# Encoder layer on one core: the norm of the tile two ahead moved in front of the copies of a tile's value product

## The chip, the cores and the metric

The kernel runs on one core of one Trainium2 chip. Its time is the device time of one execution in microseconds (us), and lower is better. A core has a matrix engine (TensorE, PE in the rows; PEld is its weight loads), VectorE (DVE), ScalarE (ACT), GpSimd (POOL), and SyncE (SP), which here only issues transfers. Each engine takes its instructions strictly in the order in which they were given to it, and waits at an instruction until what it needs is there.

## The reference

One layer of a hybrid encoder in float32, with 2048 rows of 1024 features:

```python
h = rms_norm(x, attn_norm_g)
q, k, v, xr, gr = split(h @ w_in)            # 512 columns each
attn = diff_attention(q, k, v, ...)          # 4 heads
lru  = recurrent_group(xr, gr, ...)          # RG-LRU in both directions
x = x + concat(attn, lru) @ w_out
x = x + (gelu(g) * u) @ w_down               # [g | u] = DWConv3(rms_norm(x) @ w_up)
return rms_norm(x, final_norm_g)

def rms_norm(x, g):
    return x * rsqrt(mean(x * x, axis=-1) + 1e-6) * g
```

The change is in the first line, in the `v` part of the second, and nowhere else.

## The kernel before

`phase1` computes the normed rows, their transposes, and the five projections; `phase2` is the attention, `phase3` the output projection, and the classes `Up` and `Down` the feed-forward part. The change is in the first stage of `phase1`, the value projection, which takes 16 tiles of 128 rows.

For each tile t there are four steps. `load_x(t)` fetches 128x1024 values into one of two buffers `xt`. `norm(t)` squares and sums them on ACT (L93), scales the sum on DVE (L94), raises it to the power -1/2 on POOL (L96), and multiplies `xt` in place by that and by the gain on DVE (L138). `transposed(t)` turns the normed tile with eight PE transposes (L144) and splits the result for a product in three parts: `hT_hi` on ACT (L75) and the remainder `hT_lo` on DVE (L78). `values(t)` multiplies: 8 blocks of 3 matmuls (L81 to L83) into one PSUM tile `ps`; then `vh` is copied from it on ACT (L75), `vl` is the remainder on DVE (L78), and both go to DRAM (L160).

The loop runs ahead. Half way through the product of tile t, between its fourth and fifth block, `values` calls `mid`, which is `transposed(t + 1)`. After the whole of `values(t)` comes `norm(t + 2)`. So between the transposes of tile t+1 and those of tile t+2 PE has 24 matmuls: the second half of product t and the first half of product t+1.

In this stage PE, DVE and ACT keep the order in which the code was written (`manual_schedule`, L174); SP and POOL are ordered by the scheduler. `xt` has two buffers, so the load of tile t+2 waits until the transposes of tile t have read theirs. `vl` has one buffer, so the next `vl` waits until the last one is in DRAM. The last tiles also carry the first weights of the next projection: `split_w` (a cast on DVE, L77, and a subtraction on POOL, L78).

Of the kernel before, what the change touches and what calls it, by code (L numbers as in the profile page):

```python
# [22 lines left out]
NT = S // P  # L23
# [19 lines left out]
def encoder_layer(ctx, tc, x, w_qkr, w_v, w_out, w_up, w_down, w_a, w_x, par, lams, g_attn, g_ffn, g_fin, out):  # L43
# [3 lines left out]
    def pool_of(name, **kw):  # L47
        return tc.tile_pool(name=name, reuse_waits="tile", **kw)
# [24 lines left out]
    def split(hi, lo, src, hi_eng=A, lo_eng=V):  # L73
        if hi_eng is A:
            A.activation(out=hi, in_=src, func=AF.Copy)  # L75
        else:
            hi_eng.tensor_copy(hi, src)  # L77
        lo_eng.tensor_tensor(out=lo, in0=src, in1=hi, op=ALU.subtract)  # L78

    def mm3(ps, lh, ll, rh, rl, first, last):  # L80
        T.matmul(ps, lh, rh, start=first, stop=False)  # L81
        T.matmul(ps, lh, rl, start=False, stop=False)  # L82
        T.matmul(ps, ll, rh, start=False, stop=last)  # L83

    def keep_clock(ps, n):

        for _ in range(n):
            T.matmul(ps, ident, ident, start=True, stop=True)

    def rms_norm(xt, g_b, junk, pool):  # L90

        ss = pool.tile([P, 1], F32, name="ss", tag="ss")
        A.activation(out=junk, in_=xt, func=AF.Square, accum_out=ss)  # L93
        V.tensor_scalar(out=ss, in0=ss, scalar1=1.0 / D, scalar2=EPS, op0=ALU.mult, op1=ALU.add)  # L94
        r = pool.tile([P, 1], F32, name="r", tag="r")
        G.tensor_tensor(out=r, in0=ss, in1=mhalf[:, 0:1], op=ALU.pow)  # L96
        return r


    def phase1():  # L100
# [9 lines left out]
        def fetch_w(i):  # L110
            ws = wp.tile([P, KD, P], F32, name="ws", tag="ws", bufs=1)
            nc.sync.dma_start(ws, w_qkr[i])
            return ws

        def split_w(ws):
            wh = wp.tile([P, KD, P], F32R, name="wh", tag="wh")
            wl = wp.tile([P, KD, P], F32R, name="wl", tag="wl")
            split(wh, wl, ws, hi_eng=V, lo_eng=G)
            return wh, wl

        with ExitStack() as ea:
            pa = ea.enter_context(pool_of("p1a", bufs=2, side="right"))
            pv = ea.enter_context(pool_of("p1v", bufs=1, side="right"))
            pt = ea.enter_context(pool_of("p1t", bufs=2, space=PSUM))
            g_b = pv.tile([P, D], F32, name="g_b")
            wv_hi = pv.tile([P, KD, AW], F32R, name="wv_hi")
            wv_lo = pv.tile([P, KD, AW], F32R, name="wv_lo")
            junk = pv.tile([P, D], BF16, name="junk")
            xts = {}

            def load_x(t):
                xts[t] = pa.tile([P, D], F32, name="xt", tag="xt")
                nc.sync.dma_start(xts[t], x[t * P:(t + 1) * P, :])

            def norm(t):
                xt = xts[t]
                r = rms_norm(xt, g_b, junk, pa)
                V.scalar_tensor_tensor(out=xt, in0=xt, scalar=r, in1=g_b, op0=ALU.mult, op1=ALU.mult)  # L138

            def transposed(t):  # L140
                xt = xts.pop(t)
                tp = pt.tile([P, KD, P], F32, name="tp", tag="tp")
                for k in range(KD):
                    T.transpose(tp[:, k, :], xt[:, k * P:(k + 1) * P], ident)  # L144
                c, o = divmod(t * P, CH)
                split(hT_hi[c][:, :, o:o + P], hT_lo[c][:, :, o:o + P], tp, hi_eng=A if t else V)

            def values(t, mid=None):
                c, o = divmod(t * P, CH)
                ps = pp.tile([P, AW], F32, name="ps", tag="ps")  # L150
                for k in range(KD):
                    if mid and k == KD // 2:
                        mid()
                    mm3(ps, hT_hi[c][:, k, o:o + P], hT_lo[c][:, k, o:o + P], wv_hi[:, k, :], wv_lo[:, k, :],
                        k == 0, k == KD - 1)
                vh = pa.tile([P, AW], F32R, name="vh", tag="vh")
                vl = pa.tile([P, AW], F32R, name="vl", tag="vl", bufs=1)
                split(vh, vl, ps)
                for d_, s_ in zip(v_d, (vh, vl)):
                    nc.sync.dma_start(d_[:, :, t, :], s_.bitcast(F32).rearrange("p (h e) -> p h e", h=NH))  # L160

            load_x(0)
            nc.scalar.dma_start(g_b, g_attn.partition_broadcast(P))

            staged = []
            for kk, tag in zip(range(0, KD, 2), ("wh", "wh", "wl", "ws")):
                ws = wp.tile([P, 2, AW], F32, name="wvs", tag=tag, bufs=1 if tag == "ws" else 2)
                (nc.sync, nc.scalar)[kk // 2 % 2].dma_start(ws, w_v[:, kk:kk + 2, :])
                staged.append(ws)
            load_x(1)  # L170
            nc.scalar.dma_start(prm, par)

            first = ExitStack()
            first.enter_context(tc.manual_schedule(engines={mybir.EngineType.PE, mybir.EngineType.DVE,  # L174
                                                            mybir.EngineType.Activation}))
            idle = pt.tile([P, KD, P], F32, name="tp", tag="tp")[:, 0, :]

            def wv_high(i):
                A.activation(out=wv_hi[:, 2 * i:2 * i + 2, :], in_=staged[i], func=AF.Copy)

            def wv_low(i):
                V.tensor_tensor(out=wv_lo[:, 2 * i:2 * i + 2, :], in0=staged[i], in1=wv_hi[:, 2 * i:2 * i + 2, :],
                                op=ALU.subtract)

            keep_clock(idle, 22)
            norm(0)
            wv_high(0)
            wv_low(0)
            wv_high(1)
            transposed(0)  # L190
            keep_clock(idle, 5)
            wv_high(2)
            wv_high(3)
            wv_low(1)
            norm(1)
            wv_low(2)
            wv_low(3)
            for t in range(NT):
                if t + 2 < NT:
                    load_x(t + 2)  # L200
                values(t, (lambda: transposed(t + 1)) if t + 1 < NT else None)
                if t + 2 < NT:
                    norm(t + 2)
                if t == NT - 6:
                    ws = fetch_w(8)
                if t == NT - 3:
                    ready[8] = split_w(ws)
            first.close()
# [1064 lines left out]
    class Down(Steps):  # L1273
# [128 lines left out]
        def run(self, es):  # L1402
# [19 lines left out]
            self.last_rest()  # L1422

    phase1()
    kp_stack = ExitStack()
    kp = kp_stack.enter_context(pool_of("kp", bufs=2, side="right"))
# [78 lines left out]
```

## Time and profile before

| | |
|---|---|
| median of 3 runs | 2670.63 us (2669.95 to 2675.54) |
| the profiled execution | 2676.15 us, span 2674.4 us |
| PE busy | 2588.6 us, 97% of the span |
| DVE, ACT, POOL busy | 74%, 50%, 22% |
| value projection, from the first transposes to the end of the last product | about 9.4 to 136.4 us |

The profile is of one execution on the chip. A row names the line of the kernel, the engine, the operation, and what is written and read. Matmuls are pipelined: the next one starts before the one before it has ended, and the ends shown are modelled, so the distance from start to start says more than the duration. "Idle before" is the time in which the engine had nothing to do just before a row, with what ended it.

### The profile page before, as it was taken

To read this page: it belongs to the slowest core of one execution; us is meant where nothing else is said; L and a number is where in the kernel's file an instruction comes from. 1 tells how busy PE (TensorE), PEld (TensorE's weight loads), DVE (VectorE), ACT (ScalarE), POOL (GpSimd) and SP (SyncE) were. 2 spreads that over 40 slices of the span, in tenths; PEclk is the share of its full clock that TensorE was granted. 3 is DMA by queue.
4 is the path that set the end of the run, shared out by engine and by line. 5 is a ranking of instruction groups with operands and counts; after the bars stand their busy time and mean duration, and the time that the engine had idled before them with its cause. 6 is when DMAs were issued, how large, how long until landed. Compare 5 with 4: busy or idle time off the path is not lost. (4 is left out here: it accounts for less than half of the span.)

```text
span 2674.4 us, 33695 instructions
## 1 busy us (share of the span) xinstructions
PE 2588.6 (97%) x13018; PEld 2107.5 (79%) x13018; DVE 1976.9 (74%) x2487; ACT 1342.3 (50%) x1732; POOL 588.3 (22%) x488
## 2 busy tenths in 40 slices
PE   8899999999999999999989999989999998999998
PEld 6687788778888887877768888878888886878786
DVE  4445535579999999744388888898888777675876
ACT  3334534568888888732254444454444443332433
POOL 0113223146766666810000000000000000101100
PEclk9999999999999999999999999999999999999999
DMA  5421221240202001243453434354565344755743
GB/s 170 127 81 67 85 71 63 81 158 23 88 25 87 23 25 33 80 154 126 158 173 128 148 118 157 119 168 167 221 242 205 123 140 120 202 132 125 230 157 126
DMA packets 146018, 329.36 MB, mean 123 GB/s; under 512 B 18624, under 2 KB 74688, under 8 KB 137024
## 3 DMA queue, kind: packets, MB, share of 16 engines
q1 hardware_dynamic: 133632, 283.82, 30.7%
q0 software_dynamic: 11504, 41.42, 6.3%
q8 instruction: 102, 1.67, 0.3%
q10 hardware_dynamic: 720, 1.95, 0.2%
q14 instruction: 60, 0.49, 0.1%
HBM read 198.16 MB, written 128.97 MB: 122 GB/s over the span
## 5 line engine op out<-in xcount | busy, mean ns | idle before, releaser
L1003 ACT ACTIVATE wg<-sw 128x1024 fp32r<-128x1024 f32 (+1 forms) x136 | 140.7, 1034 | 397.9 <-PE q L1029 219.2
L1044 DVE TENSOR_TENSOR u<-q,u 128x512 f32<-128x512 f32 x340 | 234.4, 690 | 138.4 <-PE q L1029 134.1
L458 ACT ACTIVATE e<-e,mn 128x2048 f32<-128x2048 f32 x128 | 256.3, 2008 | 11.9 <-DVE mn L453 11.9
L449 PE MATMUL sc<-ks,qt 64*128 64x512 f32 x1536 | 229.9, 412 | 6.9 <-DVE mn L453 6.7
L1189 DVE SCALAR_TENSOR_TENSOR acc<-u,prm,acc 128x1023 f32<-128x1023 f32 (+1 forms) x176 | 226.0, 1284 | 9.8 <-ACT acc L1181 5.4
L469 DVE SCALAR_TENSOR_TENSOR e<-e,rc,e 128x1024 f32<-128x1024 f32 x128 | 211.4, 1652 | 2.3
L83 PE MATMUL ps<-hT_hi,wl 128*128 128x512 f32 x512 | 199.5, 390 | 0.0
L82 PE MATMUL ps<-hT_lo,wh 128*128 128x512 f32 x512 | 199.5, 390 | 0.0
L81 PE MATMUL ps<-hT_hi,wh 128*128 128x512 f32 x512 | 199.5, 390 | 0.0
L449 PEld LDWEIGHTS sc<-ks,qt 64*128 64x128 f32 x1536 | 147.9, 185 | 46.7 <-DVE mn L453 10.0
L1008 DVE TENSOR_TENSOR wg<-sw,wg 128x1024 fp32r<-128x1024 f32 (+1 forms) x136 | 161.9, 1190 | 27.6 <-ACT wg L1003 27.6
L1008 DVE TENSOR_TENSOR wg<-wr,wg 128x512 fp32r<-128x512 f32 (+3 forms) x136 | 126.9, 933 | 67.1 <-ACT wg L1003 67.1
L1003 ACT ACTIVATE wg<-wr 128x512 fp32r<-128x512 f32 (+3 forms) x136 | 111.7, 822 | 117.3 <-PE q L1029 103.7
L453 DVE CUSTOM_DVE_ANT_0 e<-sc,strip,mn 128x1024 f32<-128x1024 f32 x128 | 159.1, 1281 | 15.5 <-PE sc L449 14.7
L78 POOL TENSOR_TENSOR wTl<-wg,wTh 128x1024 fp32r<-128x1024 f32 x64 | 156.9, 2451 | 0.0
L1294 POOL DMA_DIRECT2D b15f<-in_w_down_dram x1 | 0.8, 814 | 704.6 <-DVE u L1102 704.6
L453 DVE CUSTOM_DVE_ANT_0 e<-sc,strip 128x1024 f32<-128x1024 f32 x128 | 150.9, 1214 | 5.6 <-PE sc L449 3.4
L1029 PE MATMUL q<-b14r,wg 128*128 128x512 f32 x440 | 150.0, 398 | 2.9 <-ACT u L1051 2.9
L1029 PE MATMUL q<-b0r,wg 128*128 128x512 f32 x448 | 151.3, 394 | 0.7 <-DVE wg L1008 0.7
L78 POOL TENSOR_TENSOR wTl<-wf,wTh 128x512 fp32r<-128x512 f32 x64 | 126.9, 1983 | 110.4 <-ACT wTh L75 107.7
L1029 PE MATMUL q<-b12r,wg 128*128 128x512 f32 x440 | 149.7, 398 | 0.0
L475 PEld LDWEIGHTS tp<-ident,e 128*128 128x128 f32 x1024 | 112.1, 142 | 45.5 <-ACT wTh L75 18.7
(320 smaller groups left out, 6668.9 us busy)
## 6 DMA issues: line engine op xcount, KB each, us to landing
wr<-in_w_up_dram SPq DMA_DIRECT2D x66, 512.0 KB, 5.5
s_d<-sw SPq DMA_DIRECT2D x22, 1024.0 KB, 4.8
sw<-s_d SPq DMA_DIRECT2D x22, 1024.0 KB, 4.8
a_d<-acc SPq DMA_DIRECT2D x154, 128.0 KB, 1.9
x_d<-u POOLq DMA_DIRECT2D x32, 512.0 KB, 5.4
wr<-a_d SPq DMA_DIRECT2D x32, 512.0 KB, 4.8
xt<-in_x_dram SPq DMA_DIRECT2D x30, 512.0 KB, 4.7
ws<-in_w_qkr_dram SPq DMA_DIRECT2D x16, 512.0 KB, 3.4
```

Source lines behind the costliest of these rows:

```text
L78: lo_eng.tensor_tensor(out=lo, in0=src, in1=hi, op=ALU.subtract)
L81: T.matmul(ps, lh, rh, start=first, stop=False)
L82: T.matmul(ps, lh, rl, start=False, stop=False)
L449: T.matmul(self.sc[c][:, n * CH:(n + 1) * CH], l[rows, q], r[rows, kk], start=i == 0, stop=i == 2)
L453: V.tensor_tensor_reduce(out=self.e[c][:, hf * 1024:(hf + 1) * 1024], in0=self.sc[c], in1=strip[:, off:off + 1024], scale=SLOPES[self.h], ...
L458: A.activation(out=self.e[c], in_=self.e[c], func=AF.Exp, scale=-1.0, bias=self.mn[:, 2 * c + 1:2 * c + 2], accum_out=self.s[c])
L469: V.scalar_tensor_tensor(out=e0, in0=e1, scalar=self.rc, in1=e0, op0=ALU.mult, op1=ALU.add)
L1003: A.activation(out=hi, in_=src, func=AF.Copy)
L1008: V.tensor_tensor(out=lo, in0=src, in1=hi, op=ALU.subtract)
L1029: T.matmul(ps, l, r[:, k, :], start=new is not None and k == 0 and n == 0, stop=k == m - 1 and n == 2, skip_group_check=True)
L1044: V.tensor_tensor(out=out, in0=a, in1=b_, op=ALU.add)
L1189: V.scalar_tensor_tensor(out=acc[:, 0:n], in0=u[:, o + tap:o + tap + n], scalar=prm[:, C_FW + 3 * m + tap:C_FW + 3 * m + tap + 1], in1=acc ...
```

## The change

`values` takes a second function, `then`, and calls it after its 24 matmuls are issued and before `vh` and `vl`. The call of `norm(t + 2)` that stood behind `values(t)` is now that function. Operations, tiles, buffers and transfers stay the same; their order changes on ACT and DVE. On PE, SP and POOL the sequence is the same as before.

```diff
-            def values(t, mid=None):
+            def values(t, mid, then):
                 c, o = divmod(t * P, CH)
                 ps = pp.tile([P, AW], F32, name="ps", tag="ps")
                 for k in range(KD):
@@
                     mm3(ps, hT_hi[c][:, k, o:o + P], hT_lo[c][:, k, o:o + P], wv_hi[:, k, :], wv_lo[:, k, :],
                         k == 0, k == KD - 1)
+                then()
                 vh = pa.tile([P, AW], F32R, name="vh", tag="vh")
                 vl = pa.tile([P, AW], F32R, name="vl", tag="vl", bufs=1)
                 split(vh, vl, ps)
@@
-                values(t, (lambda: transposed(t + 1)) if t + 1 < NT else None)
-                if t + 2 < NT:
-                    norm(t + 2)
+                values(t, (lambda: transposed(t + 1)) if t + 1 < NT else None,
+                       (lambda: norm(t + 2)) if t + 2 < NT else lambda: None)
```

ACT in the middle of the stage, before. `tp_521` and `tp_571` are the transposes of tiles 6 and 7, `ps_508` and `ps_558` the products of tiles 5 and 6, `xt_506` and `xt_556` the rows of tiles 7 and 8:

```order
L75 ACTIVATE hT_hi1_161<-tp_521 128x8x128
L75 ACTIVATE vh_544<-ps_508 128x512
L93 ACTIVATE junk_180,ss_550<-xt_506 128x1024
L75 ACTIVATE hT_hi1_161<-tp_571 128x8x128
L75 ACTIVATE vh_594<-ps_558 128x512
L93 ACTIVATE junk_180,ss_600<-xt_556 128x1024
```

ACT at the same place, now:

```order
L75 ACTIVATE hT_hi1_161<-tp_521 128x8x128
L93 ACTIVATE junk_180,ss_544<-xt_506 128x1024
L75 ACTIVATE vh_550<-ps_508 128x512
L75 ACTIVATE hT_hi1_161<-tp_571 128x8x128
L93 ACTIVATE junk_180,ss_594<-xt_556 128x1024
L75 ACTIVATE vh_600<-ps_558 128x512
```

The square of tile 8's rows (`xt_556`) stood behind the copy of product 6 (`ps_558`); it now stands in front of it, right behind `hT_hi` of tile 7.

DVE at the same place, before:

```order
L78 TENSOR_TENSOR hT_lo1_165<-tp_571,hT_hi1_161 128x8x128
L78 TENSOR_TENSOR vl_595<-ps_558,vh_594 128x512
L94 TENSOR_SCALAR ss_600<-ss_600 128x1
L138 SCALAR_TENSOR_TENSOR xt_556<-xt_556,r_603,g_b_177 128x1024
L78 TENSOR_TENSOR hT_lo2_166<-tp_621,hT_hi2_162 128x8x128
```

DVE at the same place, now:

```order
L78 TENSOR_TENSOR hT_lo1_165<-tp_571,hT_hi1_161 128x8x128
L94 TENSOR_SCALAR ss_594<-ss_594 128x1
L138 SCALAR_TENSOR_TENSOR xt_556<-xt_556,r_597,g_b_177 128x1024
L78 TENSOR_TENSOR vl_601<-ps_558,vh_600 128x512
L78 TENSOR_TENSOR hT_lo2_166<-tp_621,hT_hi2_162 128x8x128
```

The two DVE steps of the norm of tile 8 moved in front of `vl` of product 6.

DVE at the end of the stage, before (`ps_910`, `ps_962` and `ps_1004` are the products of tiles 13, 14 and 15, `ws_806` and `ws_1220` weights of the next projections):

```order
L94 TENSOR_SCALAR ss_952<-ss_952 128x1
L138 SCALAR_TENSOR_TENSOR xt_908<-xt_908,r_955,g_b_177 128x1024
L77 CAST wh_958<-ws_806 128x1024
L78 TENSOR_TENSOR hT_lo3_167<-tp_975,hT_hi3_163 128x8x128
L78 TENSOR_TENSOR vl_999<-ps_962,vh_998 128x512
L77 CAST wh_1222<-ws_1220 128x1024
L78 TENSOR_TENSOR vl_1030<-ps_1004,vh_1029 128x512
```

DVE at the same place, now:

```order
L138 SCALAR_TENSOR_TENSOR xt_908<-xt_908,r_949,g_b_177 128x1024
L78 TENSOR_TENSOR vl_953<-ps_910,vh_952 128x512
L77 CAST wh_958<-ws_806 128x1024
L78 TENSOR_TENSOR hT_lo3_167<-tp_975,hT_hi3_163 128x8x128
L77 CAST wh_1222<-ws_1220 128x1024
L78 TENSOR_TENSOR vl_999<-ps_962,vh_998 128x512
L78 TENSOR_TENSOR vl_1030<-ps_1004,vh_1029 128x512
```

Here `vl` of product 13 stands between the last norm and the first cast, and the second cast, which the scheduler places, has come in front of `vl` of product 14.

## Rows read from the trace of the kernel before

**Rows 1.** The page's first part: engine, busy us, share of the span, instructions.

```profile
PE 2588.6 (97%) x13018; PEld 2107.5 (79%) x13018; DVE 1976.9 (74%) x2487; ACT 1342.3 (50%) x1732; POOL 588.3 (22%) x488
```

**Rows 2.** Waits of PE over the span: total us, times, longest; the first row.

```profile
PE tp L144 <- DVE xt L138: 18.4, 16, 1.2
```

**Rows 3.** The same view, 22 to 128 us alone.

```profile
PE tp L144 <- DVE xt L138: 17.0, 14, 1.2
```

**Rows 4.** Stretches: length, busy us of PE, PEld, DVE, ACT, POOL, clock, DMA share, GB/s.

```profile
22.98:126.84 103.86, 86.85 (x419) 68.27 (x417) 45.05 (x54) 34.59 (x52) 7.27 (x14) 1.00 0.44 131
136.40:180.00 43.60, 43.60 (x193) 35.83 (x192) 19.43 (x48) 8.46 (x16) 4.18 (x4) 1.00 0.25 79
```

**Rows 5.** Timeline of PE, one period: start us, duration us, what, idle before.

```profile
62.29 0.39 PE L83 MATMUL ps<-wv_hi,hT_lo 128*128 128x512 f32 x1
63.91 1.06 PE L144 MATMUL tp<-ident,xt 128*128 128x128 f32 x8 [1.22 <-DVE xt L138]
64.72 0.47 PE L81 MATMUL ps<-wv_hi,hT_hi 128*128 128x512 f32 x1
...
70.16 0.39 PE L83 MATMUL ps<-wv_hi,hT_lo 128*128 128x512 f32 x1
71.77 1.06 PE L144 MATMUL tp<-ident,xt 128*128 128x128 f32 x8 [1.22 <-DVE xt L138]
```

**Rows 6.** Timeline of ACT in that period.

```profile
65.00 1.03 ACT L75 ACTIVATE hT_hi<-tp 128x1024 fp32r<-128x1024 f32 x1 [3.44 <-PE tp L144]
67.79 0.60 ACT L75 ACTIVATE vh<-ps 128x512 fp32r<-128x512 f32 x1 [1.76 <-PE ps L83]
68.29 1.05 ACT L93 ACTIVATE junk<-xt 128x1024 bf16<-128x1024 f32 x1
```

**Rows 7.** Timeline of DVE in that period.

```profile
66.06 1.23 DVE L78 TENSOR_TENSOR hT_lo<-tp,hT_hi 128x1024 fp32r<-128x1024 f32 x1 [2.31 <-ACT hT_hi L75]
68.42 0.69 DVE L78 TENSOR_TENSOR vl<-ps,vh 128x512 fp32r<-128x512 f32 x1 [1.14 <-ACT vh L75]
69.46 0.15 DVE L94 TENSOR_SCALAR ss<-ss 128x1 f32<-128x1 f32 x1 [0.34 <-ACT junk L93]
70.34 1.29 DVE L138 SCALAR_TENSOR_TENSOR xt<-xt,r,g_b 128x1024 f32<-128x1024 f32 x1 [0.73 <-POOL r L96]
```

**Rows 8.** Timeline of PE in the attention: transposes behind a matmul without a wait.

```profile
699.61 0.39 PE L449 MATMUL sc<-ks,qt 64*128 64x512 f32 x1
699.94 1.09 PE L475 MATMUL tp<-ident,e 128*128 128x128 f32 x8
```

**Rows 9.** Timeline of PE, the first of the 14 waits.

```profile
22.98 0.40 PE L83 MATMUL ps<-wv_hi,hT_lo 128*128 128x512 f32 x1
24.50 1.09 PE L144 MATMUL tp<-ident,xt 128*128 128x128 f32 x8 [1.13 <-DVE xt L138]
```

**Rows 10.** Timeline of PE, the last of the 14 waits.

```profile
125.23 0.39 PE L83 MATMUL ps<-wv_hi,hT_lo 128*128 128x512 f32 x1
126.84 1.06 PE L144 MATMUL tp<-ident,xt 128*128 128x128 f32 x8 [1.22 <-DVE xt L138]
```

**Rows 11.** Timeline of SP, transfers issued in that period.

```profile
65.00 0.33 SPq L133 DMA_DIRECT2D xt<-in_x_dram  x1
...
69.14 0.51 SPq L160 DMA_DIRECT2D v_d<-vl  x1
```

**Rows 12.** From issue to landing, transfers of `xt`, 0 to 140 us.

```profile
DMA to landing us min/median/max: 3.2/3.4/10.8
```

**Rows 13.** From issue to landing, transfers of `vh` and `vl`, 20 to 130 us.

```profile
DMA to landing us min/median/max: 2.6/2.7/3.5
```

**Rows 14.** Timeline of DVE at the end of the stage.

```profile
133.20 0.69 DVE L77 CAST wh<-ws 128x1024 fp32r<-128x1024 f32 x1 [1.15 <-DMA ws<-in_w_qkr_dram]
136.96 0.69 DVE L78 TENSOR_TENSOR vl<-ps,vh 128x512 fp32r<-128x512 f32 x1 [3.06 <-ACT vh L75]
```

**Rows 15.** Timeline of ACT, the first copy of the next projection.

```profile
141.79 0.60 ACT L289 ACTIVATE xr<-ps 128x512 f32<-128x512 f32 x1 [3.29 <-PE ps L83]
```

## The prediction

> **What bounds the kernel now.** I read the page's shares first: PE is busy 97% of the span, so a change pays where PE stands still, and only there [rows 1]. The waits of PE come next. The longest item of the whole list is the one that this change touches: 18.4 us in 16 waits of the transposes (L144) for the normed tile (DVE L138) [rows 2]. Restricted to 22 to 128 us it is 17.0 us in 14 waits, 1.2 us each [rows 3]; these 14 are the transposes of tiles 2 to 15. The stretch from the last matmul before the first of these waits to the last of them is 103.86 us long, and PE is busy in 86.85 us of it, at a granted clock of 1.00, that is 2.4 GHz [rows 4]. No other engine is full there either: PEld has 68.27, DVE 45.05, ACT 34.59 us. It is a latency chain that holds PE, not the amount of work of any engine.
>
> The timeline shows the chain. In the period that begins with the transposes of tile 7 (63.91 us), the last matmul before the next transposes starts at 70.16 and those start at 71.77: 1.61 us from start to start [rows 5]. ACT has finished `hT_hi` of tile 7 at 65.00 + 1.03 = 66.03 and then does nothing until 67.79, when product 6 is complete and `vh` can be copied; only behind that copy, at 68.29, does it square the rows of tile 8 [rows 6]. From that square to the transposes of tile 8 it is 71.77 - 68.29 = 3.48 us, through the sum on DVE at 69.46, the power on POOL and the scaling on DVE at 70.34 [rows 5 to 7]. Nothing in these 3.48 us needs product 6. The square stands behind the copy by its place in the queue alone.
>
> **The change part by part.** Nothing is removed or added. Two things are moved.
>
> First, on ACT the square goes ahead of `vh`. Its input must be there: the load of a tile is issued 1.09 us after the transposes of the tile two before it (65.00 against 63.91), and lands in 3.4 us in the median [rows 11, 12]. For tile 9, issued at 65.00, that is 68.4, and its square comes a whole period later, so the rows are not what is late. The square of tile 8 can then start where `hT_hi` ends. As the rows overlap by a tenth of a microsecond (68.29 against 67.79 + 0.60), this is at about 65.93, instead of 68.29: 2.36 us earlier [rows 6]. The sum on DVE comes 1.17 us behind the square's start now (69.46 - 68.29) and would be due at 67.10, but DVE is in `hT_lo` until 66.06 + 1.23 = 67.29 and takes it then [rows 7]. From the sum to the transposes it is 71.77 - 69.46 = 2.31 us, so tile 8 would be ready for PE at 67.29 + 2.31 = 69.60.
>
> Secondly, how early can PE take it? Its last matmul of the first half starts at 70.16. In the attention, transposes that wait for nothing start 0.33 us behind the start of a 512-column matmul [rows 8]. So PE comes at 70.16 + 0.33 = 70.49, and the tile has been ready for 0.89 us. The wait is gone whole, and what is late next is PE itself. A period shrinks from 7.86 us (71.77 - 63.91) to 6.58.
>
> The sum goes by start to start. Each wait gives 1.61 - 0.33 = 1.28 us, as in the last [rows 10]; the first is shorter, 1.52 - 0.33 = 1.19 us [rows 9]. That makes 1.19 + 13 x 1.28 = 17.8 us. The bounds are near: by the idle time that the profile itself counts up to modelled ends it is 17.0 us [rows 3]; if transposes could follow at the average distance of the matmuls, (70.16 - 64.72) / 23 = 0.24 us [rows 5], it would be 1.28 + 13 x 1.37 = 19.1 us. I take 17.8, since its 0.33 us is the one row that shows this very change from matmul to transposes unhindered.
>
> The profile's figure of 1.22 us idle is thus smaller than what PE loses, because the matmul before it is drawn until 70.16 + 0.39. The Trainium skill bears on that ("TensorE: Matmul & The Clock Gate", section "Back-to-back issue gap"): a warm matmul of N columns holds the array for N / 2.4 GHz plus about 2.5 ns, 216 ns at 512 columns, and its longer latency overlaps the next one. By that figure the wait would be worth 1.52 - 0.22 + 13 x (1.61 - 0.22) = 19.4 us, where the row with the 0.33 us says 17.8; the rows' own distance of 0.24 us already lies above the rule's 0.22.
>
> What is pushed back by the move: `vl` of product 6, which stood in front of the sum and now stands behind the scaling. The scaling would end at 70.34 + 1.29 - 69.46 = 2.17 us after 67.29, at 69.46, and `vl` lasts 0.69 us, so its transfer is issued at 70.15 instead of 69.14 [rows 7, 11]. Three things hang on it, and I cost them at nothing. `hT_lo` of tile 8 is the next on DVE; it starts 66.06 - 63.91 = 2.15 us after its transposes, that is at 70.49 + 2.15 = 72.64, when DVE has long been free. The next load of rows is behind that transfer on SP, but waits for the transposes of tile 8 until 70.49 + 1.09 = 71.58 anyway; an issue takes 0.51 us. And the one buffer of `vl` is written again a period later, while the transfer lands in 2.7 us, 3.5 at most [rows 13]. `vh` itself is not late: product 6 is complete at 67.79, and the square with its read-out has ended by 65.93 + 1.17 = 67.10. If one of these covers failed, PE would feel it only beyond the 0.89 us of slack.
>
> At the end of the stage the second weight cast comes ahead of `vl` of product 14. The cast waits for weights; it starts 133.20 - 126.84 = 6.36 us after the last transposes, and `vl` of 14 would end some 1.4 us later, at 7.75 on that scale. Its transfer lands 2.7 us later, at 10.5; `vl` of product 15, in the same buffer, starts at 136.96 - 126.84 = 10.12 before, so it slips by about 0.4 us [rows 10, 13, 14]. Behind it on DVE is preparation of the next projection, of which ACT needs the first part at 141.79, over 4 us after `vl` ended [rows 14, 15]. Bounds: nothing, or 0.4 us if that slack did not count. I take nothing.
>
> After the stage PE has no gap at all from 136.40 to 180.00, 43.60 us of 43.60 [rows 4]. All that follows starts from PE's products, so the whole rest moves forward by what the stage gives.
>
> The sum against the profiled execution: 2676.15 - 17.8 = 2658.3 us. That execution lies 5.5 us above the median of the runs, 2670.63; from the median it is 2652.8 us, and that is the forecast. It is 0.67% less. A change below 0.2%, 5.3 us here, could not be told from none.
>
> **The rivals.** One: the load of the rows becomes the bound, and the kernel is slower. With two buffers a tile's load is issued 1.09 us after the transposes of the tile two before, lands after L, and its own transposes start 3.48 us behind the landing. Two periods then last 1.09 + L + 3.48, and one lasts (4.57 + L) / 2. PE's own 6.58 us is exceeded from L = 8.6 on, and the present 7.86 from L = 11.2 on; every further microsecond costs half a microsecond for each of 13 tiles. For it speaks that loads will be issued right behind the later `vl` transfer, and that one load did take 10.8 us [rows 12]; with the 2.7 us of a transfer queued ahead, L = 13.5 would give a period of 9.04 us and 13 x 1.18 = 15 us more, 2686 us. Against it: 10.8 is the slowest of all 16, which include those issued at the start together with the weights, and the median is 3.4. In the stage the transfer engines are busy 0.44 of the time [rows 4]; the same bytes in 84% of the time make 0.53.
>
> Two: a wait remains. If the square could not start at the end of `hT_hi`, or DVE came to the sum later, each microsecond beyond the 0.89 of slack comes back 13 times. A square later by 1.5 us would leave about 0.6 us a tile, a gain of 17.8 - 8 = 10 us, 2661 us. Against it: all the times of that chain are rows.
>
> Three: the stage gains, but a later one gives it back, since DVE or a transfer there keeps its own time. Then it is about 2670 us, no change. Against it speaks the gapless PE after the stage; for it only that later stages also wait, for reasons that the move may shift.
>
> That the move does nothing is excluded as far as order goes: on ACT and DVE the norm does stand in front.
>
> **How the numbers follow.** The forecast, the wait gone whole: 0.87. A remaining wait with a gain above 5.3 us: 0.06. Given back, or a gain within 0.2%: 0.04. Slower by the loads: 0.03. Faster is thus 0.93, same 0.04, slower 0.03. The forecast's own bounds are 2670.6 - 19.1 = 2651.5 and 2670.6 - 17.0 = 2653.6; the runs of before spread from 0.7 below to 4.9 above their median, and small shifts in later stages can add a few to either side. That makes 2648 to 2659, which leaves the remaining wait mostly outside.
>
> **What would show it.** In the profile of the changed kernel the wait of L144 for L138 should be gone but for the first two, about 1.4 us of 18.4; the transposes should follow at 6.6 us, 0.33 us behind a matmul; the square should start at the end of `hT_hi`, and `vl` right after the scaling; the stage should end near 118.6 us instead of 136.4. Wrong would be a PE that still waits for L138, a square that waits for a transfer, or a stage shorter by 17 us with the same end.

## The result, and the profile after

The changed kernel took 2650.52 us in the median of 4 runs (2648.49 to 2653.84), the kernel before 2671.48 us (4 runs, 2669.95 to 2675.54): ratio 0.992, 95% interval 0.9903 to 0.9938, 21 us less. Five further rounds put the ratio at 0.9927 (0.9914 to 0.994), that is 19.5 us less.

The page's first part of after (busy us, share, instructions), answering [rows 1]:

```profile
PE 2583.5 (98%) x13018; PEld 2107.9 (80%) x13018; DVE 1976.1 (75%) x2487; ACT 1341.9 (51%) x1732; POOL 586.3 (22%) x488
```

Every engine has the same number of instructions as before. PE's busy time is 5.1 us less, and 2.55 of these lie in the stretch shown below: a matmul that is followed at once counts until the next start (0.23 us), one in front of a wait until its modelled end (0.39 us). What went is waiting. The list of PE's waits over the span (total us, times, longest), where the line of [rows 2] has fallen from 18.4 us in 16 waits to the two at the head of the stage:

```profile
PE tp L144 <- DVE xt L138: 1.6, 2, 1.0
```

The stretch from the last matmul before the first of the 14 transposes to the last of these transposes (length, busy us of PE, PEld, DVE, ACT, POOL, clock, DMA share, GB/s), answering [rows 4]:

```profile
23.07:107.37 84.30, 84.30 (x418) 69.38 (x417) 41.64 (x53) 34.66 (x52) 7.14 (x13) 1.00 0.55 159
```

It was 103.86 us long with PE busy in 86.85; now it is 84.30 us, with PE busy in all of it. The granted clock is 1.00 in both. The same bytes take less time, so the DMA share rose from 0.44 to 0.55.

One period on PE (start, duration, what), answering [rows 5], then the last transposes, answering [rows 10]:

```profile
55.41 0.39 PE L83 MATMUL ps<-wv_hi,hT_lo 128*128 128x512 f32 x1
55.64 1.03 PE L144 MATMUL tp<-ident,xt 128*128 128x128 f32 x8
...
61.87 0.39 PE L83 MATMUL ps<-wv_hi,hT_lo 128*128 128x512 f32 x1
62.10 1.04 PE L144 MATMUL tp<-ident,xt 128*128 128x128 f32 x8
...
107.14 0.39 PE L83 MATMUL ps<-wv_hi,hT_lo 128*128 128x512 f32 x1
107.37 1.03 PE L144 MATMUL tp<-ident,xt 128*128 128x128 f32 x8
```

The transposes start 0.23 us behind the last matmul, where it was 1.61. The period is 6.46 us, where it was 7.86, and the last transposes start at 107.37 instead of 126.84: the stage is 19.47 us shorter. (The stretch above is 19.56 us shorter, because it begins 0.09 us later, at 23.07 instead of 22.98.)

ACT in that period, answering [rows 6]:

```profile
56.71 1.03 ACT L75 ACTIVATE hT_hi<-tp 128x1024 fp32r<-128x1024 f32 x1 [3.07 <-PE tp L144]
57.63 1.05 ACT L93 ACTIVATE junk<-xt 128x1024 bf16<-128x1024 f32 x1
...
59.50 0.60 ACT L75 ACTIVATE vh<-ps 128x512 fp32r<-128x512 f32 x1 [0.73 <-PE ps L83]
```

DVE, answering [rows 7]:

```profile
57.77 1.23 DVE L78 TENSOR_TENSOR hT_lo<-tp,hT_hi 128x1024 fp32r<-128x1024 f32 x1 [2.57 <-ACT hT_hi L75]
58.91 0.14 DVE L94 TENSOR_SCALAR ss<-ss 128x1 f32<-128x1 f32 x1
59.78 1.28 DVE L138 SCALAR_TENSOR_TENSOR xt<-xt,r,g_b 128x1024 f32<-128x1024 f32 x1 [0.73 <-POOL r L96]
60.98 0.68 DVE L78 TENSOR_TENSOR vl<-ps,vh 128x512 fp32r<-128x512 f32 x1
```

The square starts where `hT_hi` ends and the sum where `hT_lo` ends, without idle time before either. Before, the scaling was followed by its transposes 1.43 us later (70.34, 71.77). By that the tile is ready at 59.78 + 1.43 = 61.21, and PE comes at 62.10: 0.89 us of slack. `vl` now follows the scaling directly.

The transfers of `xt` from issue to landing, 0 to 140 us, answering [rows 12], then from 20 us on:

```profile
DMA to landing us min/median/max: 3.6/3.7/10.9
```

```profile
DMA to landing us min/median/max: 3.6/3.7/4.1
```

Those of `vh` and `vl`, 15 to 120 us, answering [rows 13]; the 5.2 is the last of them, issued at 118.19 in the next stage:

```profile
DMA to landing us min/median/max: 2.5/2.6/5.2
```

In the median loads take 0.3 us longer than before. The 10.9 belongs to one issued at the start, as the 10.8 of before did; from 20 us on the slowest takes 4.1, far from the 8.6 at which loads would have decided.

### The profile page after: what moved, and what is told of

Its sections match the earlier page's. It is cut to its first block, busy times and chain, and to the rows that moved or that the text cites. A ratio compares the mean times of both kernels' runs of the same rounds, so it can differ in the third digit from the quotient of the medians.

```text
span 2646.7 us, 33694 instructions
## 1 busy us (share of the span) xinstructions
PE 2583.5 (98%) x13018; PEld 2107.9 (80%) x13018; DVE 1976.1 (75%) x2487; ACT 1341.9 (51%) x1732; POOL 586.3 (22%) x488
## 5 line engine op out<-in xcount | busy, mean ns | idle before, releaser
L475 PEld LDWEIGHTS tp<-ident,e 128*128 128x128 f32 x1024 | 110.6, 141 | 45.2 <-ACT wTh L75 18.7
```

## The experiments

Every kernel was timed beside the kernel before on the same chip. The first four shared one chip (before: 2672.97 us, 21 runs), the last three another (2673.2 us, 18 runs). Medians scatter by a few microseconds, so the stage's length in the trace is given beside each ratio.

### The kernel before once more, and the changed one in five rounds

No edit. 

> The kernel before once more, for a second profile of it. The traces of before and after differ by 27.7 us over the span, of which 19.5 us are there when the value projection ends; the other 8.2 us come little by little until the end. Theory: that rest is scatter between executions of one program, since the profiled execution of before was a slow one (2676 us, median 2671) and that of after a fast one (2648 us, median 2651). Then this second profile ends its value projection within 0.3 us of the first, at the same times row by row, but reaches its end some us away from the first one. Rival: the rest is a lasting gain that the shift brings to later stages; then both profiles of before agree at every stage within about 1 us, and 2674 us is the span again.

> The changed kernel against the one before in five rounds. Theory (the stage's gain and nothing else): 19.5 us less, ratio 0.9927. Rival (later stages gain too, as the two traces taken by themselves would have it): 27 us less, ratio 0.990.

The second profile of before shows the same stage: 17.0 us in 14 waits, last transposes at 127.5 (first profile: 127.6). After that the two run apart. The norm in the output projection (L758: count, duration ns, first and last start, form), in the first and the second profile of before:

```profile
L758 DVE SCALAR_TENSOR_TENSOR xt<-xt,r,g_b x14: 1274/1284/1287, 1174.4 to 1335.9; 128x1024 f32<-128x1024 f32 x14
```

```profile
L758 DVE SCALAR_TENSOR_TENSOR xt<-xt,r,g_b x14: 1277/1284/1286, 1171.1 to 1329.8; 128x1024 f32<-128x1024 f32 x14
```

In the first and the second profile of the changed kernel:

```profile
L758 DVE SCALAR_TENSOR_TENSOR xt<-xt,r,g_b x14: 1276/1284/1286, 1150.1 to 1308.9; 128x1024 f32<-128x1024 f32 x14
```

```profile
L758 DVE SCALAR_TENSOR_TENSOR xt<-xt,r,g_b x14: 1277/1285/1286, 1151.2 to 1310.1; 128x1024 f32<-128x1024 f32 x14
```

One and the same program differs by 6.1 us at that place (1335.9, 1329.8) and by 3.6 at its end (spans 2674.4, 2670.8); the changed one by 1.2 (spans 2646.7, 2647.9). The five rounds give 0.9927, the theory's figure; the 0.990 of a lasting gain in later stages lies outside the interval. So the 8.2 us by which the first two traces differ beyond the stage are largely scatter. That the shift is worth a microsecond or two later on is not excluded, since the interval is 7 us wide.

### Half of the change: the square alone

The norm is split into `square` (ACT) and `scale` (the sum, the power and the scaling). The edit is to the changed kernel; the part that defines the two functions is left out here.

```diff
-                       (lambda: norm(t + 2)) if t + 2 < NT else lambda: None)
+                       (lambda: square(t + 2)) if t + 2 < NT else lambda: None)
+                if t + 2 < NT:
+                    scale(t + 2)
```

> Half of the change: only the square on ACT goes ahead of the copy vh; the two DVE steps of the norm stay behind vl. Theory (the path is the last of two queues: square on ACT and vl on DVE): the sum on DVE can then come directly behind vl, 0.61 us after vl starts (68.42), at 69.03 instead of 69.46; the period falls from 7.86 to about 7.43 us, some 6 us less, 2665 us, and PE waits still about 0.8 us at each of the transposes. Rival (ACT's order alone held the chain): the whole 19.5 us, 2651 us, with no wait left.

Measured: 2670.09 us, ratio 0.9983 (0.9973 to 0.9993), by which it is 4.5 us less (2.9 by the two medians), where 6 were expected. DVE, then PE, then the wait in the list (the split norm's lines are L143, L146, L156 in this kernel):

```profile
65.92 0.69 DVE L78 TENSOR_TENSOR vl<-ps,vh 128x512 fp32r<-128x512 f32 x1 [1.14 <-ACT vh L75]
66.53 0.14 DVE L143 TENSOR_SCALAR ss<-ss 128x1 f32<-128x1 f32 x1
```

```profile
67.66 0.40 PE L83 MATMUL ps<-wv_hi,hT_lo 128*128 128x512 f32 x1
68.83 1.06 PE L156 MATMUL tp<-ident,xt 128*128 128x128 f32 x8 [0.77 <-DVE xt L146]
```

```profile
PE tp L156 <- DVE xt L146: 10.9, 14, 0.8
```

The sum stands 0.61 us behind the start of `vl` and PE still waits, 0.8 us a tile. The last transposes come 5.9 us earlier than before (121.7, against 127.6), as expected. The median is 2670 and not 2665 all the same; 6 us less lies inside the ratio's interval (1.9 to 7.2), and the trace of the stage, not the median, is what bears the reading. ACT's order alone did not hold the chain.

### The other half: the steps on DVE alone

The edit is again to the changed kernel.

```diff
-                then()
                 vh = pa.tile([P, AW], F32R, name="vh", tag="vh")
                 vl = pa.tile([P, AW], F32R, name="vl", tag="vl", bufs=1)
-                split(vh, vl, ps)
+                A.activation(out=vh, in_=ps, func=AF.Copy)
+                then()
+                V.tensor_tensor(out=vl, in0=ps, in1=vh, op=ALU.subtract)
```

> The other half: on DVE the two steps of the norm go ahead of vl, while on ACT the square stays behind the copy vh. Theory: the sum waits for the square anyway (DVE idled 0.34 us before it), so nothing is gained: 2671 us, within 2 us, with the same wait of 1.2 us. Rival (vl in front of the sum held the chain): most of 19.5 us, 2651 to 2660 us.

Measured: 2675.87 us, ratio 1.001 (1.0 to 1.0019). The wait of PE, then the sum on DVE:

```profile
PE tp L144 <- DVE xt L138: 17.0, 14, 1.2
```

```profile
69.38 0.15 DVE L94 TENSOR_SCALAR ss<-ss 128x1 f32<-128x1 f32 x1 [2.17 <-ACT junk L93]
```

DVE now has nothing in front of the sum, and idles 2.17 us there for the square. The wait is the 17.0 us of before, and the last transposes are at 127.6 as before. Alone this half gives nothing; the two halves gave 5.9 and 0 us of the 19.5 in the stage. The 0 to 5 us that the ratio allows on the slow side have no place in the stage, and I leave them open.

### One and two squares more: how much slack is there

The edit is to the changed kernel; the second kernel has a 2 in place of the 1 before `if`.

```diff
             def norm(t):
                 xt = xts[t]
+                for _ in range(1 if t > 1 else 0):
+                    A.activation(out=junk, in_=xt, func=AF.Square)
                 r = rms_norm(xt, g_b, junk, pa)
```

> The changed kernel with one more square of the same rows on ACT ahead of the one that counts, for tiles 2 to 15 (its result is thrown away). Theory (the normed tile is ready 0.89 us before PE comes for it: in the trace of after the scaling starts at 59.78, the tile would be taken 1.43 us later, at 61.21, and the transposes start at 62.10): the extra square puts the sum 0.84 us later, just inside that slack, so 2651 us, at most 2 us more. Rival (there is no such slack, the chain and PE only happen to meet): 0.84 us in each of 14 tiles, 12 us more, 2662 us.

> The same with two more squares. Theory: the sum comes 1.79 us later, 0.90 us beyond the slack, so the wait of PE is back in each of 14 tiles: 12.6 us more than the changed kernel, 2663 us. Rival (the chain is far from PE's path, so that ACT's work here does not matter at all): 2651 us. Rival (no slack at all): 25 us more, 2676 us.

One more: 2653.49 us, ratio 0.9929 (0.9916 to 0.9941), the changed kernel's own figure. PE in it, then the sum on DVE:

```profile
63.20 1.06 PE L146 MATMUL tp<-ident,xt 128*128 128x128 f32 x8
...
69.47 0.40 PE L83 MATMUL ps<-wv_hi,hT_lo 128*128 128x512 f32 x1
69.86 1.06 PE L146 MATMUL tp<-ident,xt 128*128 128x128 f32 x8
```

```profile
67.54 0.15 DVE L94 TENSOR_SCALAR ss<-ss 128x1 f32<-128x1 f32 x1 [0.96 <-ACT junk L93]
```

The transposes follow at 0.39 us instead of 0.23, though no idle time is printed: a wait of 0.16 us lies inside the modelled end of the matmul. The sum comes 67.54 - 63.20 = 4.34 us behind the transposes, where it was 58.91 - 55.64 = 3.27. That is 1.07 later, not the expected 0.84, and so 0.18 beyond the slack of 0.89 instead of just inside it. The period is 69.86 - 63.20 = 6.66 us, 0.20 more, and the stage's last transposes are 2.5 us later than with the change alone (110.6, 108.1). 2.5 us is too little for the ratio to tell.

Two more: 2669.77 us, ratio 0.9992 (0.9983 to 1.0001), which misses the 2663 us of the theory and both rivals. ACT, DVE and PE of one period:

```profile
65.16 2.14 ACT L138 ACTIVATE junk<-xt 128x1024 bf16<-128x1024 f32 x2
67.39 1.06 ACT L93 ACTIVATE junk<-xt 128x1024 bf16<-128x1024 f32 x1
```

```profile
68.57 0.15 DVE L94 TENSOR_SCALAR ss<-ss 128x1 f32<-128x1 f32 x1 [2.05 <-ACT junk L93]
```

```profile
63.13 1.06 PE L146 MATMUL tp<-ident,xt 128*128 128x128 f32 x8 [1.11 <-DVE xt L140]
70.88 1.07 PE L146 MATMUL tp<-ident,xt 128*128 128x128 f32 x8 [1.10 <-DVE xt L140]
```

The two squares put the third back by 67.39 - 65.16 = 2.23 us, 1.11 each, not the 0.95 that I had taken. The sum then comes 68.57 - 63.13 = 5.44 us behind the transposes, where it was 3.27: 2.17 later. Less the slack of 0.89 that is 1.28 us a tile, and the period grew by 7.75 - 6.46 = 1.29. So the slack holds to within 0.02 us, and the price of a square was the error: 13 x 1.29 = 17 us instead of 12.6. The stage agrees: its last transposes are at 125.9, 17.8 us later than with the change alone. Of the rivals, "no slack" would have been 25 us by my own price, and 13 x 2.17 = 28 by the measured one.

### Before, with the transposes one block later

```diff
-                    if mid and k == KD // 2:
+                    if mid and k == 5:
```

> The kernel before, with its order on ACT and DVE, but the transposes of the next tile stand behind the fifth block of a product instead of the fourth, so PE has 15 matmuls instead of 12 between a product's end and the transposes. Theory (the wait is a distance: a tile is ready 3.98 us after its square's copy starts, and PE comes too early): three more matmuls of 0.23 us cover 0.70 us of the wait; the period falls from 7.86 to about 7.17 us, 9.7 us less, 2662 us, with some 0.5 us of idle time left. Rival (PE's place in the product does not matter, since hT_lo of the next tile then comes too late for the next product): no gain, 2671 us.

Measured: 2664.13 us, ratio 0.9966 (0.9954 to 0.9978), 9.1 us less. The wait and one period of PE:

```profile
PE tp L144 <- DVE xt L138: 6.1, 14, 0.5
```

```profile
61.13 1.06 PE L144 MATMUL tp<-ident,xt 128*128 128x128 f32 x8 [0.44 <-DVE xt L138]
...
68.30 1.06 PE L144 MATMUL tp<-ident,xt 128*128 128x128 f32 x8 [0.44 <-DVE xt L138]
```

The period is 7.17 us, to the hundredth what was expected, and ACT's first copy of the next projection comes 9.0 us earlier (132.81, against 141.79 in [rows 15]). The loss was a distance between two events, a product's end and the next transposes, and it shrinks as well when PE is given more to do between them.

## Why the prediction was right

**The wait goes whole.** Right: 14 waits are gone, and PE is what comes last. The two queues had to be changed together, as the halves show.

**The slack of 0.89 us.** Right: it was worked out as 70.49 - 69.60 and read after as 62.10 - 61.21, and the kernels with more squares lose what exceeds it, to within 0.02 us a tile. That both figures are the same to the hundredth is luck, since two errors cancel. PE comes 62.10 - 55.64 = 6.46 us after the transposes before, not 6.58; and the tile is ready 61.21 - 55.64 = 5.57 us after them, not 5.69, mainly because the sum starts 1.14 us behind the start of `hT_lo` (58.91 - 57.77), where the prediction waited for its shown end, 1.23.

**The sum of 17.8 us.** Its size was low by 1.7 us; the stage gave 19.47, which is also above my upper bound of 19.1. The mis-sized term was the 0.33 us from a matmul to transposes [rows 8]. Measured it is 0.23, the ordinary distance of two matmuls here. That is 14 x 0.10 = 1.4 us; a further 13 x 0.03 = 0.4 comes from the transposes themselves, which hand on to the next matmul after 0.79 us instead of 0.82 (62.89 - 62.10, against [rows 5]), and was in none of the bounds. The 0.09 by which the stretch begins later is lost again.

It was not "the one row that shows this very change", as the prediction says. The trace of before has the same pair of shapes without a wait in its output projection, where a 512-column matmul on 128 rows (128*128) stands in front of eight such transposes:

```profile
1193.74 0.39 PE L83 MATMUL po<-wo,cl 128*128 128x512 f32 x1
1193.97 1.03 PE L766 MATMUL tp<-ident,xt 128*128 128x128 f32 x8
1194.76 0.48 PE L81 MATMUL po<-wo,ch 128*128 128x512 f32 x1
```

Here it is 0.23 us to the transposes, as in all 13 such places of that stage, and 0.79 from them to the next matmul. With these two figures the sum would have been (1.52 - 0.23) + 13 x (1.61 - 0.23 + 0.03) = 19.6 us, against the 19.56 of the stretch. So the size could have been read before anything ran.

The row that I took was a poor neighbour. The matmul in front of its transposes is the last of a run of 12 that have 64 rows each (64*128), as PE's timeline of before shows:

```profile
698.34 1.67 PE L449 MATMUL sc<-ks,qt 64*128 64x512 f32 x12
```

In the trace they start two at a time, 0.23 us from pair to pair (698.91, 699.14, 699.38, 699.61): two of them seem to run side by side. Why the step from there to transposes is 0.33 us was not tested by itself.

The Trainium skill ("TensorE: Matmul & The Clock Gate", section "Back-to-back issue gap") gives the 216 ns for 512 columns as the gap of a single matmul in isolation, and about 131 ns for a stream of weight loads and matmuls, which the prediction leaves out. This stage is such a stream, and its trace has 0.23 us from start to start: a little more than the first figure, and far from the second. That the 19.4 us worked out from 216 ns lies so near to 19.5 is partly luck, since it takes 0.22 for 0.23 and leaves out the 0.03 of the transposes.

**Nothing lost by later copies.** Right. SP's transfers in that period, answering [rows 11]:

```profile
55.23 0.51 SPq L161 DMA_DIRECT2D v_d<-vl  x1
56.70 0.33 SPq L133 DMA_DIRECT2D xt<-in_x_dram  x1
```

The transfer of `vl` now goes out 0.41 us before the transposes at 55.64, where it was 2.63 us before them (69.14, 71.77), and the load behind it is still issued 1.06 us after the transposes (1.09 before).

**The end of the stage.** Right to take nothing for it, though the slip of 0.4 us that was worked out did not come. DVE (the second cast, `vl` of products 14 and 15), then ACT's first copy of the next projection, answering [rows 14, 15]:

```profile
113.36 0.69 DVE L77 CAST wh<-ws 128x1024 fp32r<-128x1024 f32 x1 [2.64 <-DMA ws<-in_w_qkr_dram]
113.97 0.68 DVE L78 TENSOR_TENSOR vl<-ps,vh 128x512 fp32r<-128x512 f32 x1
117.47 0.69 DVE L78 TENSOR_TENSOR vl<-ps,vh 128x512 fp32r<-128x512 f32 x1 [2.81 <-ACT vh L75]
```

```profile
122.30 0.60 ACT L289 ACTIVATE xr<-ps 128x512 f32<-128x512 f32 x1 [3.29 <-PE ps L83]
```

`vl` of product 15 waits for `vh` and not for its buffer: it starts 117.47 - 107.37 = 10.10 us after the last transposes, 10.12 before. The cast came sooner than I had put it, 113.36 - 107.37 = 5.99 us after the last transposes and not 6.36, so the transfer of `vl` 14, issued at 114.69, lands 2.6 us later at 117.29, 0.18 us before the buffer is wanted. The copy at 122.30 is 19.49 us earlier than at 141.79, so the stage ends near 116.9, where 118.6 was expected.

**The rivals.** The load of the rows never came near: 3.7 us in the median and 4.1 at most from 20 us on, against 8.6. A remaining wait did not occur by itself; with one square more a period is 0.20 us longer, and with two 1.29. That later stages give the gain back is excluded by the five rounds.

**The level.** The forecast of 2652.8 lies 2.3 us above the median of the first four runs and 0.6 below that of the five rounds. Of the 2.3, the mis-sized term explains 1.7; the rest is within the scatter. That the five rounds come so near is luck: their kernel before stood at 2672.97, 2.3 us above the 2670.63 from which the forecast started, which hides the gain that was too low.

## What to carry to other kernels

Where engines take their work in order, an instruction whose input is early should not stand behind one whose input is late: look in the timeline for an engine that idles until X and then runs Y, where Y does not need X. Follow the chain through every queue, since here half the move gave 5.9 us, the other half nothing, and both 19.5. Size the gain from start to start of matmuls at their own distance, not from the printed idle time and not from a matmul of another shape; search the whole trace for the same pair of shapes first.

## What was not expected of the hardware

A wait of up to 0.16 us in front of a matmul prints no idle time at all, because the modelled end of the one before (0.39 us for a start-to-start distance of 0.23) covers it; only the starts show it.

Squares of 128x1024 on ACT that write the same scratch tile follow each other at 1.11 us (2.23 for two, with two squares more), while the square behind `hT_hi`, which writes another tile, follows at 0.92 (57.63 - 56.71), though both last 1.03 to 1.06. That the common tile is the reason was not tested.
